# A hybrid attention and pooling layer on one core: the first output product of the last unit moved between two projections, and five stages' row factors sent through memory

## The chip, the cores and the metric

The kernel runs on one core of a Trainium2 chip. The metric is device microseconds of one execution. Three runs of the kernel before took 1174.0, 1173.38 and 1174.05 us; the median is 1174.0.

## What is computed

One layer on x of 4096 tokens by 1024 channels, in fp32. Normalised x goes through one combined projection into q, k, v, two gates and the input of a pooling group. The q, k, v feed attention of 8 query heads (2 key heads) inside a band of 128 tokens to both sides, with a learned bias and a sink. Attention and pooling, each times its gate, are joined and go through the output projection, whose normalised result is added to x. The core of the reference:

```python
h = rmsnorm(x, pre_norm_g[l])
proj = jnp.einsum('bsd,de->bse', h, w_in[l])
q, k, v, g_a, u_p, g_p = jnp.split(proj, splits, axis=-1)
...
a = banded_attention(q, k, v, rel_bias, attn_sink[l]) * jax.nn.silu(g_a)
p = multiscale_pool(u_p, pool_w[l], pool_scale[l]) * jax.nn.silu(g_p)
mixed = jnp.einsum('bse,ed->bsd', jnp.concatenate([a, p], axis=-1), w_out[l])
x = x + rmsnorm(mixed, post_norm_g[l])
```

with `rmsnorm(x, g) = x * rsqrt(mean(x*x) + eps) * g`. The factor rsqrt(...) is one number per token, here called the row factor.

## The kernel before

**Precision.** An fp32 operand is carried as two fp16 pieces, a high one and a low one (the rest). A product of two such operands takes three matmuls: high by high, high by low, low by high. "Low" instructions on VectorE or POOL make the second piece by a subtraction. The large products are further cut by a scheme of seven products for eight (names "11", "12", "22" for plain products, "s1" to "s4" for products of sums).

**Phase 1, up to about 481 us.** The tokens are cut into 8 stages of 512. The stages' steps (loads, squares, factors, operands, products) are put into a list by `do` and `ld`, each with an engine, a guessed duration and a due key, and `Steps.run` (line 78) orders them: at each point it takes the engine that is free first and, of the steps ready there, the one with the smallest due key. The order that comes out is the program's order on each engine. `prepare(m)` (line 968) adds what stage m needs before its products: four blocks of x with tokens on partitions are loaded, ScalarE squares and sums them (`square`), POOL takes the power −1/2 (`root`, into `rs4`, 128 tokens by 4 columns), TensorE spreads the factor (`spread_all`, line 445): x for the products is loaded with channels on partitions, so the factor has to stand along the free axis of all 128 partitions, and four fp32 products of `rs4`'s columns with a unit matrix bring it there, in PSUM. Then `norm` on VectorE multiplies x by gain and factor, and `x_operands` splits the result.

**Phase 2, from 481 us.** Units of 256 tokens are walked downward, 15 to 0 (`U` = 15 is the last unit of the sequence, the first to be done), and blocks of 128 tokens, 31 to 0, with them. `due(t, fn, ...)` collects all steps with a time written by hand; sorted by that time they are issued, and each engine works through its own in that order. The opening, unit 15, is written as one table of TensorE's steps and lists for the others (from line 1815); `at_` counts from the opening's start.

The steps that matter here, b a block, half one of two groups of heads, u a unit:

- `proj_k`, `proj_v`, `proj_q` (u): projections on TensorE; `keep_k`, `keep_v`, `keep_q`: ScalarE writes the high half, VectorE the low half (line 1230).
- `scores(b, half)` on TensorE; then `soft` places `logits` (VectorE, line 1308), `exps` (ScalarE, 1319), `denominators` (VectorE, 1326 and 1329), `probs` (ScalarE, 1341) and `rests` (VectorE, 1349), which write the tile `pn`, and `turn` (line 1358), a DMA transpose of `pn` into `pt` issued on SP.
- `values(b)` (line 1451) multiplies `pt` of half 0 and then of half 1 with the values `vv`; each half needs its own transpose.
- `gate(b)` (VectorE, 1475) takes the result out of PSUM; `sum1`, `sum3`, `sum2` (VectorE, 1536 to 1542) build the operands of the products of sums.
- `product(u, name, o, tag)` (line 1601) is one of the output products; its operand comes from `cast` (ScalarE and POOL, 1503 and 1507). `begin` (ScalarE, 1619) copies "11" out of its bank before "12" adds into it; `gain11` (VectorE, 1629) reads that bank last, and "s2" then overwrites it.
- Loads on SP: `load_wo` (1671), `pool_in` (1530), `load_ga` (1432), `load_xr` (1648), `load_x` (1226).

All of the DMAs of phase 2 are issued by SP, in its program order.

Of the kernel before, what the change touches and what calls it, by code (L numbers as in the profile page):

```python
# [8 lines left out]
F32 = mybir.dt.float32  # L9
# [8 lines left out]
P = 128  # L18
# [3 lines left out]
T = 512  # L22
NM = S // T
NB = S // P
# [15 lines left out]
O11, O12, O21, O22, OT1, OT2, OT4, OT3 = range(8)  # L40
# [16 lines left out]
class Steps:  # L57
# [28 lines left out]
    def run(self):  # L86
        n_steps = len(self.steps)
        users = [[] for _ in range(n_steps)]
        open_deps = []
        for n, s in enumerate(self.steps):  # L90
            open_deps.append(len(s[5]))
            for d in s[5]:
                users[d].append(n)
        ready = [0.0] * n_steps
        begun = [None] * n_steps
        free = dict.fromkeys(("PE", "DVE", "ACT", "POOL", "SP"), 0.0)
        dma_free = 0.0
        waiting = {e: [] for e in free}
        for n in range(n_steps):
            if not open_deps[n]:  # L100
                waiting[self.steps[n][0]].append(n)
        left = n_steps
        while left:
            best = None
            for e, ns in waiting.items():
                if ns:
                    t = max(free[e], min(ready[n] for n in ns))
                    if best is None or t < best[0]:
                        best = (t, e)
# [25 lines left out]
def hybrid_layer(ctx: ExitStack, tc, io, out):  # L135
    nc = tc.nc
# [4 lines left out]
    dram = ctx.enter_context(tc.tile_pool(name="dram", bufs=1, space=DRAM))  # L141
# [8 lines left out]
    mhalf = const.tile([P, 1], F32, name="mhalf")  # L150
# [12 lines left out]
    gs = const.tile([P, 1], F32, name="gs")  # L163
# [10 lines left out]
    epss = const.tile([P, 1], F32, name="epss")  # L174
    psc = const.tile([P, 4], F32, name="psc")

    f_row = dram.tile([NH, 512], F32, name="f_row")
    f_scr = dram.tile([NH, FR + 1, NF], F32, name="f_scr")
    x_scr = dram.tile([NU, P, 2, 2, HK, UT], F16, name="x_scr")
# [30 lines left out]
    with ExitStack() as actx:  # L210
        pa = actx.enter_context(tc.tile_pool(name="pa", bufs=1))
# [8 lines left out]
        ident = pa.tile([P, P], F32, name="ident")  # L220
        onesf = pa.tile([P, P], F32, name="onesf")
        edge = pa.tile([P, 4, 16], F32, name="edge")
        rs4 = pa.tile([P, 4], F32, name="rs4")
        xn1 = pa.tile([P, D], F32, name="xn")
        sqt = [pa.tile([P, D], BF16, name=f"sq{i}") for i in range(2)]
        ssq = [pa.tile([P, 4], F32, name=f"ssq{i}") for i in range(2)]
# [73 lines left out]
        V, G, A = nc.vector, nc.gpsimd, nc.scalar  # L300
# [61 lines left out]
        bc = {}  # L362
# [76 lines left out]
        def spread(m, i):  # L439
            nc.tensor.matmul(  # L440
                bc[m][:, i * P : (i + 1) * P], rs4[:, i : i + 1].to_broadcast([P, P]), ident,
                start=True, stop=True, skip_group_check=True,
            )

        def spread_all(m):
            bc[m] = psa.tile([P, T], F32, name=f"bc{m}", tag=f"wup{m % 2}")
            for i in range(4):
                spread(m, i)

        def n_view(m, c):  # L450
            return NT[:, (c % 2) * D : (c % 2 + 1) * D].rearrange("p (b t) -> p b t", b=2)
# [47 lines left out]
        for c in range(HK):  # L499
            do("ACT", act(512), -5 + 0.1 * c, first_square, c,  # L500
               r=[f"n0.{c}.0"], w=[f"xsq{c}"])
# [450 lines left out]


        def pads():
            V.memset(ubuf[:, :, 0:16], 0.0)
            V.memset(ubuf[:, :, T + 16 : T + 24], 0.0)

# [7 lines left out]
        sum_weights(UU, sw[:, 8:9], "u4", M1 + 8, 3.0, "DVE")  # L965
        sum_weights(GA, sw[:, 4:5], "a4", M1 + 27, 3.0, "DVE")

        def prepare(m):
            key = start(m) - 55
            b = m % 2  # L970
            for i in range(4):
                xn, k = (xn1, "xn") if m > 1 or i % 2 == 0 else (NT[:, 2 * D : 3 * D], "ts")
                t = key - 9 + 3 * i if m > 1 else 20 + i
                ld(t - 3, xn, x_blk[BPM * m + i], 0.5, w=[k])
                do("ACT", 1.3, t, square, m, i, xn, w=[k, f"ssq{m % 2}.{i}"])
            do("POOL", 1.0, key + 3, root, m, slice(0, 4), r=[f"ssq{m % 2}.{i}" for i in range(4)] + ["mhalf"],
               w=["rs4", "rs0", "rs1"])
            do("PE", 1.2, key + 5, spread_all, m, r=["rs4", "ident"], w=[f"wup{m % 2}"])
            for c in range(HK):
                k = key + 14 + 9 * c  # L980
                n = f"n1.{c % 2}"
                ld(k - 9, n_view(m, c), xT[c][:, :, m], 0.5,
                   w=[n] + ([f"xsq{i}" for i in range(HK)] if m == 1 and c < 2 else []))
                for h in range(2):
                    do("DVE", dve(512), k + h, norm, m, c, h, r=["gs", f"wup{m % 2}"], w=[n])
                x_operands(m, c, k + 2, "DVE")
            if m < NM - 1:
                for u in range(2):
                    do("SP", 0.45, key + 55 + 4 * u,
                       lambda u=u: nc.sync.dma_start(x_scr[2 * m + u], xb[b][:, u]),  # L990
                       r=xkeys(m, "b"), dma=3.5)
# [796 lines left out]
    for t, fn, *args in (  # L1788
        (0.0, proj_k, U, 2),
        (2.6, proj_v, U),  # L1790
        (5.4, proj_q, U, 0, 0),
        (10.8, proj_q1, U, 1, 0, 1),
        (13.5, scores, NB - 1, 0),
        (14.3, proj_q1, U, 1, 1, 1),
        (17.0, proj_k, U - 1, 2),
        (19.7, scores, NB - 1, 1),
        (20.6, proj_v, U - 1),
        (23.4, proj_q1, U - 1, 0, 0, 0),
        (26.1, scores, NB - 2, 0),
        (27.2, proj_q1, U - 1, 0, 1, 0),  # L1800
        (29.9, proj_q1, U - 1, 1, 0, 1),
        (32.6, scores, NB - 2, 1),
        (33.7, proj_q1, U - 1, 1, 1, 1),
        (36.4, values, NB - 1, 0),
        (38.4, product, U, "22", OT4, 2),
        (41.0, scores, NB - 3, 0),
        (42.0, proj_k, U - 2, 1),
        (44.7, proj_v, U - 2),
        (47.5, scores, NB - 3, 1),
        (48.4, product, U, "11", O11, 0),  # L1810
        (51.1, values, NB - 2, 1),
        (53.1, product, U, "12", O21, 0, True),
        (55.7, scores, NB - 4, 0),
        (56.7, proj_q, U - 2, 0, 1),
        (62.1, product, U, "s2", OT2, 0),
        (64.7, values, NB - 3, 1),
        (66.7, scores, NB - 4, 1),
        (67.6, proj_q, U - 2, 1, 0),
        (73.0, product, U, "s3", OT3, 1),
        (75.6, product, U, "s1", OT1, 0),  # L1820
    ):
        at_(t, fn, *args)
# [3 lines left out]
    soft(NB - 2, 0, 27.2, 27.8, 31.1, 31.6, 32.2, 34.5)  # L1826
    soft(NB - 2, 1, 34.4, 35.0, 38.3, 38.8, 39.4, 41.7)
    soft(NB - 3, 0, 42.0, 42.6, 45.9, 46.4, 47.0, 49.3)
    soft(NB - 3, 1, 50.1, 50.7, 54.0, 54.5, 55.1, 57.4)
    soft(NB - 4, 0, 59.4, 60.0, 63.2, 63.7, 64.3, 67.0)  # L1830
    softmax(NB - 4, 1, 67.6)

# [10 lines left out]
    at_(38.35, keep_q, U - 1, 1)  # L1843
    at_(38.37, gate, NB - 1)
    cast(41.0, 41.6, U, "11", a11, G)
    at_(46.3, keep_k, U - 2)
    at_(47.2, keep_v, U - 2)
    at_(50.5, begin, U)
    at_(53.1, gate, NB - 2)
    at_(53.2, sum1, U)  # L1850
    at_(54.1, sum3, U)
    at_(57.1, sum2, U)
    cast(58.0, 58.7, U, "s2", a11, G)
    at_(58.1, square, U, 0, 0, 0)
# [256 lines left out]
```

## Time and profile before

| | |
|---|---|
| profiled execution | 1173.47 us |
| its span, first to last instruction | 1171.7 us |
| mean granted TensorE clock | 0.998 |
| TensorE busy | 1154.8 us, 14420 matmuls |
| VectorE, ScalarE, POOL busy | 935.8, 703.3, 312.5 us |

Times in rows are microseconds from the span's start unless marked ns. PE is TensorE, PEld its weight loads, DVE VectorE, ACT ScalarE, SP the engine that issues the DMAs. In a row of the timeline stand start, duration, engine, line, operation, tiles written and read, shapes and how many like it follow in a piece; in brackets how long the engine stood idle before it and what ended that. An L with a number is a line of the kernel before.

### The profile page before, as it was taken

The numbers are of one execution on the slowest core, as the hardware profiler recorded it, in microseconds if no ns is written. First come the engines' busy times: TensorE is split into PE (matmuls) and PEld (weight loads), VectorE is DVE, ScalarE is ACT, GpSimd is POOL, SyncE is SP. The second block draws the span as 40 slices with busy tenths as digits, with TensorE's granted clock in tenths as the row PEclk, the third lists the DMA queues.
The fourth block names the chain that finished last, engine by engine and source line by source line (L and its number), as shares of the span: only waits on it lengthen the run. The fifth ranks groups of instructions, "written<-read, shape, count | busy, mean of one in ns | idle before, by whom it ended". The sixth has DMA issues, their size and how long they took to land. (4 is left out here: it accounts for less than half of the span.)

```text
span 1171.7 us, 34178 instructions
## 1 busy us (share of the span) xinstructions
PE 1154.8 (99%) x14420; PEld 889.6 (76%) x14420; DVE 935.8 (80%) x1864; ACT 703.3 (60%) x1460; POOL 312.5 (27%) x310
## 2 busy tenths in 40 slices
PE   7999999999999999999999999999999999999997
PEld 6998888998888888886667676676666767767643
DVE  6889997798688984558978877977787787797787
ACT  6876555557454542256676666666667666666672
POOL 0002111110110100201534433532543443353231
PEclk9999999999999999999999999999999999999999
DMA  9545587679457474299975886786787587686684
GB/s 345 211 126 183 168 268 245 181 250 289 155 176 243 149 195 137 74 279 229 250 183 138 197 202 134 198 187 183 164 190 180 139 200 197 133 196 161 175 213 145
DMA packets 291290, 224.67 MB, mean 192 GB/s; under 512 B 210576, under 2 KB 249744, under 8 KB 286528
## 3 DMA queue, kind: packets, MB, share of 16 engines
q1 hardware_dynamic: 291136, 222.48, 69.6%
q8 instruction: 113, 1.85, 0.7%
q14 instruction: 41, 0.34, 0.1%
HBM read 113.37 MB, written 60.33 MB: 148 GB/s over the span
## 5 line engine op out<-in xcount | busy, mean ns | idle before, releaser
L669 PEld LDWEIGHTS <-wq 128*128 128x128 f16 x4104 | 401.0, 98 | 53.0 <-issue 3.3
L669 PE MATMUL y<-xt,wq 128*128 128x256 f16 x1512 | 203.8, 273 | 0.1
L1319 ACT ACTIVATE p<-p,nm 128x385 f32<-128x385 f32 (+1 forms) x256 | 152.8, 599 | 36.3 <-POOL p L1302 20.4
L1240 PE MATMUL aq<-xb,xb 128*128 128x256 f16 x1024 | 173.4, 273 | 0.1
L1601 PE MATMUL ms<-wo,ys 128*128 128x512 f16 x720 | 162.7, 379 | 0.3 <-DVE mo L1640 0.3
L1349 DVE SCALAR_TENSOR_TENSOR pn<-p,rd,pn 128x384 f16<-128x384 f32 (+1 forms) x256 | 157.3, 665 | 5.9 <-ACT pn L1341 5.9
L1308 DVE CUSTOM_DVE_ANT_0 p<-s,nt,nsink 128x384 f32<-128x384 f32 (+1 forms) x256 | 155.9, 665 | 1.8 <-PE s L1285 1.7
L1240 PEld LDWEIGHTS <-xb 128*128 128x128 f16 x1280 | 125.2, 98 | 22.5 <-issue 6.3
L1240 PE MATMUL aq<-xb,xt 128*128 128x256 f16 x512 | 139.6, 273 | 0.0
L1341 ACT ACTIVATE pn<-p,rd 128x384 f16<-128x384 f32 (+1 forms) x256 | 134.5, 596 | 4.0 <-issue 1.1
L1601 PEld LDWEIGHTS <-ys 128*128 128x128 f16 x720 | 69.2, 98 | 81.6 <-issue 2.9
L1601 PE MATMUL m<-wo,y 128*128 128x512 f16 x540 | 121.8, 379 | 0.0
L304 POOL TENSOR_TENSOR yt<-yt,sg 128x512 f32<-128x512 f32 (+2 forms) x32 | 49.7, 1554 | 265.6 <-DVE yt L307 215.0
L1601 PEld LDWEIGHTS <-y 128*128 128x128 f16 x540 | 51.4, 98 | 63.4 <-issue 3.1
L1635 POOL TENSOR_TENSOR mo<-mo,gpost 128x512 f32<-128x512 f32 x39 | 63.8, 1635 | 94.6 <-ACT jkb L1624 93.4
L669 PE MATMUL plain<-xb,wq 128*128 128x256 f16 x576 | 67.0, 273 | 3.9 <-DVE wq L307 2.4
L1240 PEld LDWEIGHTS <-xt 128*128 128x128 f16 x640 | 62.6, 98 | 8.7 <-issue 0.4
L669 PE MATMUL v<-xt,wq 128*128 128x256 f16 x504 | 68.6, 273 | 0.6 <-DVE cc L304 0.6
L669 PE MATMUL x<-xb,wq 128*128 128x256 f16 x504 | 68.4, 273 | 0.6 <-DVE ubuf L307 0.5
L669 PE MATMUL y<-xb,wq 128*128 128x256 f16 x504 | 68.8, 273 | 0.0
L669 PE MATMUL v<-xb,wq 128*128 128x256 f16 x504 | 68.6, 273 | 0.0
L1451 PEld LDWEIGHTS <-vv 128*64 128x64 f16 (+1 forms) x2256 | 55.1, 109 | 12.2 <-issue 8.0
(214 smaller groups left out, 1935.3 us busy)
## 6 DMA issues: line engine op xcount, KB each, us to landing
nt<-in_xT SPq DMA_DIRECT2D x28, 512.0 KB, 4.7
x_scr<-xb SPq DMA_DIRECT2D x14, 1024.0 KB, 7.0
xb<-x_scr SPq DMA_DIRECT2D x14, 1024.0 KB, 7.4
xr<-in_x SPq DMA_DIRECT2D x28, 512.0 KB, 4.5
out<-xr SPq DMA_DIRECT2D x28, 512.0 KB, 2.6
xn<-in_x SPq DMA_DIRECT2D x27, 512.0 KB, 5.1
ga_scr<-cc SPq DMA_DIRECT2D x64, 128.0 KB, 3.1
raw<-in_w_out SPq DMA_DIRECT2D x16, 512.0 KB, 4.9
```

Of the source, the lines that this page charges most:

```text
L304: eng.tensor_tensor(out=out, in0=in0, in1=in1, op=op)
L669: nc.tensor.matmul(b[:, s], wq[:, slot[q, op], wv, s, k, :], x[:, xv, k, :], start=(first and k + s + wv + xv == 0), stop=(last and k == H ...
L1240: nc.tensor.matmul(acc, w[:, j, k, :], x[:, kh, v, kt, :], start=(n == 0), stop=(n == 3 * KT - 1),)
L1308: nc.vector.tensor_tensor_reduce(out=p_t[b, half][:, hh, :nk], in0=s_t[jj][:, gg, :nk], in1=bias[:, h, lo : lo + nk], scale=negc[:, h : h ...
L1319: nc.scalar.activation(p[:, hh, : nk + 1], p[:, hh, : nk + 1], AF.Exp, bias=nm_t[b, half][:, hh : hh + 1], scale=-1.0, accum_out=den_t[b, ...
L1341: nc.scalar.activation(prob_view(b, half)[:, 0, i], p_t[b, half][:, i, :nk], AF.Copy, scale=rd_t[b, half][:, i : i + 1],)
L1349: nc.vector.scalar_tensor_tensor(out=pn4[:, 1, i], in0=p_t[b, half][:, i, :nk], scalar=rd_t[b, half][:, i : i + 1], in1=pn4[:, 0, i], op0= ...
L1451: nc.tensor.matmul(o_t[b][side][a, half], v_t[ku][ks, vi, kt, a], pt[b, half][ks, pi, g, :, kb - kbs[0], (LOW, TOP)[side]], start=start, s ...
L1601: nc.tensor.matmul(z_t[u, tag], y[:, k, yi, :], wo[o][:, wi, k, :], start=(n == 0 and acc is None), stop=(n == 3 * HK - 1), skip_group_che ...
L1635: eng.tensor_tensor(out=mo, in0=mo, in1=gpost[:, cs], op=ALU.mult)
```

## The change

It has two parts.

The first: for stages 3 to 7 (`MS` = 3) `spread_all` is left out. In its place VectorE copies `rs4` into four columns of a tile of 128x32 and transposes it in blocks of 32x32, SP stores the four rows of each block into a scratch row in memory (four DMAs) and loads that row broadcast to all partitions (one DMA) into `rows`, one SBUF tile; `norm` reads it in place of the PSUM tile. The loads of x blocks, squares and root of these stages have due keys 20 us earlier. For the latency of the two transfers the planner gets an engine "NET" with steps of 12 and 8 us that issue nothing.

The second: in unit 15's opening product "11" goes between `proj_k` and `proj_v` of unit 13, product "12" ahead of `values` of block 30, and the steps of ScalarE, VectorE and SP near them get other times.

```diff
@@ class Steps, run
-        free = dict.fromkeys(("PE", "DVE", "ACT", "POOL", "SP"), 0.0)
+        free = dict.fromkeys(("PE", "DVE", "ACT", "POOL", "SP", "NET"), 0.0)
@@ phase 1
+        def rows_turn(m):
+            V.tensor_copy(turned[0][:, :4], rs4)
+            V.transpose(out=turned[1], in_=turned[0])
+
+        def rows_store(m):
+            for i in range(4):
+                nc.sync.dma_start(
+                    rs_scr[m, i * P : (i + 1) * P].rearrange("(r c) -> r c", c=32),
+                    turned[1][i::32, :],
+                )
+
+        def rows_load(m):
+            bc[m] = rows
+            nc.sync.dma_start(
+                rows, rs_scr[m].rearrange("(o t) -> o t", o=1).to_broadcast([P, T])
+            )
@@ pads
+            V.memset(turned[0], 0.0)
@@ prepare
-                t = key - 9 + 3 * i if m > 1 else 20 + i
+                t = key - 9 - early + 3 * i if m > 1 else 20 + i
...
-            do("PE", 1.2, key + 5, spread_all, m, r=["rs4", "ident"], w=[f"wup{m % 2}"])
+            if m < MS:
+                spread_key = f"wup{m % 2}"
+                do("PE", 1.2, key + 5, spread_all, m, r=["rs4", "ident"], w=[spread_key])
+            else:
+                spread_key = "rsp"
+                do("DVE", 0.5, key - 12, rows_turn, m, r=["rs4"], w=["turned"])
+                do("SP", 1.8, key - 12, rows_store, m, r=["turned"], w=["rs_scr"])
+                do("NET", 12.0, key - 12, lambda: None, w=["rs_scr"])
+                do("SP", 0.45, key - 8, rows_load, m, r=["rs_scr"], w=["rsp"])
+                do("NET", 8.0, key - 8, lambda: None, w=["rsp"])
@@ unit 15, the table of TensorE
         (42.0, proj_k, U - 2, 1),
-        (44.7, proj_v, U - 2),
-        (47.5, scores, NB - 3, 1),
-        (48.4, product, U, "11", O11, 0),
-        (51.1, values, NB - 2, 1),
-        (53.1, product, U, "12", O21, 0, True),
+        (44.7, product, U, "11", O11, 0),
+        (47.3, proj_v, U - 2),
+        (50.1, scores, NB - 3, 1),
+        (51.0, product, U, "12", O21, 0, True),
+        (53.6, values, NB - 2, 1),
         (55.7, scores, NB - 4, 0),
@@ unit 15, the others (soft: times of logits, exps, denominators, probs, rests, turn)
-    soft(NB - 3, 1, 50.1, 50.7, 54.0, 54.5, 55.1, 57.4)
+    soft(NB - 3, 1, 51.1, 51.7, 55.0, 55.5, 56.1, 58.4)
...
-    at_(46.3, keep_k, U - 2)
-    at_(47.2, keep_v, U - 2)
-    at_(50.5, begin, U)
-    at_(53.1, gate, NB - 2)
-    at_(53.2, sum1, U)
-    at_(54.1, sum3, U)
+    at_(47.4, begin, U)
+    at_(50.1, keep_k, U - 2)
+    at_(50.2, keep_v, U - 2)
+    at_(55.7, gate, NB - 2)
+    at_(55.75, sum1, U)
+    at_(56.5, sum3, U)
```

The loads near there keep their times:

```python
at_(49.4, load_ga, NB - 3)
at_(57.5, load_wo, OT1)
at_(57.6, load_wo, O22)
at_(58.0, pool_in, U - 1, 0)
at_(58.1, load_ga, NB - 4)
at_(58.2, load_xr, U, 1)
at_(58.2, load_xr, U, 0)
```

What this does to the order is seen at two places. The first is SP in unit 15's opening, from the transpose of block 29, half 0, on (`pt29_0` is that transpose's target, `wo` a weight block, `yf` pooling's result, `gb` a gate, `xr` a block of x for the residual). In the kernel before:

```order
L1358 DMA_TRANSPOSE pt29_0_7037<-pn29_0_6964 128x24x128
L1432 DMA gb29_7039<-ga_scr_96 128x512
L1358 DMA_TRANSPOSE pt29_1_7259<-pn29_1_7152 128x24x128
L1671 DMA wo4_6065<-w_scr_98 128x4096
L1671 DMA wo3_6064<-w_scr_98 128x4096
L1530 DMA yf0_14_7265<-yp_scr_95 128x512
L1432 DMA gb28_7269<-ga_scr_96 128x512
L1648 DMA xr30_7272<-in_x 128x1024
L1648 DMA xr31_7274<-in_x 128x1024
L1358 DMA_TRANSPOSE pt28_0_7449<-pn28_0_7309 128x24x128
```

In the changed kernel (whose lines are 33 further on):

```order
L1391 DMA_TRANSPOSE pt29_0_7003<-pn29_0_6942 128x24x128
L1465 DMA gb29_7005<-ga_scr_97 128x512
L1704 DMA wo4_6080<-w_scr_99 128x4096
L1704 DMA wo3_6079<-w_scr_99 128x4096
L1563 DMA yf0_14_7278<-yp_scr_96 128x512
L1465 DMA gb28_7282<-ga_scr_97 128x512
L1681 DMA xr30_7285<-in_x 128x1024
L1681 DMA xr31_7287<-in_x 128x1024
L1391 DMA_TRANSPOSE pt29_1_7289<-pn29_1_7161 128x24x128
L1391 DMA_TRANSPOSE pt28_0_7464<-pn28_0_7324 128x24x128
```

The transpose of block 29, half 1, has moved from ahead of six loads to behind them.

The second place is VectorE at the same time: from the reciprocals of (29,1) to `gain11` (`at30` the gated block 30, `s1_15` the result of sum1, `mo15_0` that of `gain11`). Before:

```order
L1475 SCALAR_TENSOR_TENSOR at30_7144<-o30_7054,gaf_78,gb30_6730 128x4x64
L1475 SCALAR_TENSOR_TENSOR at30_7144<-p30_7053,gaf_78,gb30_6730 128x4x64
L1536 TENSOR_TENSOR s1_15_7147<-at30_7144,yf0_15_6101 128x512
L1326 TENSOR_SCALAR den29_1_7042<-den29_1_7042 128x4
L1329 RECIPROCAL rd29_1_7043<-den29_1_7042 128x4
L1539 TENSOR_TENSOR at30_7144<-at30_7144,at31_6795 128x512
L1349 SCALAR_TENSOR_TENSOR pn29_1_7152<-p29_1_7044,rd29_1_7043,pn29_1_7152 128x384 x4
L1542 TENSOR_TENSOR at31_6795<-s1_15_7147,at31_6795 128x512
L1629 TENSOR_TENSOR mo15_0_7047<-m11_15_7023,gpost_6069 128x512
```

After:

```order
L1359 TENSOR_SCALAR den29_1_7073<-den29_1_7073 128x4
L1362 RECIPROCAL rd29_1_7074<-den29_1_7073 128x4
L1508 SCALAR_TENSOR_TENSOR at30_7211<-o30_7085,gaf_78,gb30_6745 128x4x64
L1508 SCALAR_TENSOR_TENSOR at30_7211<-p30_7084,gaf_78,gb30_6745 128x4x64
L1569 TENSOR_TENSOR s1_15_7214<-at30_7211,yf0_15_6116 128x512
L1382 SCALAR_TENSOR_TENSOR pn29_1_7161<-p29_1_7075,rd29_1_7074,pn29_1_7161 128x384
L1572 TENSOR_TENSOR at30_7211<-at30_7211,at31_6810 128x512
L1382 SCALAR_TENSOR_TENSOR pn29_1_7161<-p29_1_7075,rd29_1_7074,pn29_1_7161 128x384
L1575 TENSOR_TENSOR at31_6810<-s1_15_7214,at31_6810 128x512
L1382 SCALAR_TENSOR_TENSOR pn29_1_7161<-p29_1_7075,rd29_1_7074,pn29_1_7161 128x384 x2
L1662 TENSOR_TENSOR mo15_0_6994<-m11_15_6927,gpost_6084 128x512
```

The two gates and the three sums, of which two gates and a sum stood ahead of the reciprocals and one sum behind pn, now all stand between the reciprocals and the last pn. Ahead of these rows, the low halves of unit 13's keys and values (one before the first and one before the second of the four pn of (29,0)) now follow all four pn of (29,0), ahead of the logits of (29,1).

In phase 1 SP's order at the first of the changed stages, stage 3, becomes (`rs_scr` the scratch row; `ga_scr` and `yp_scr` results of phase 1, `x_scr` operands of x, `nt` and `xn` loads of x):

```order
L459 DMA rs_scr_92<-turned1_117 4x32 x4
L890 DMA yp_scr_96<-yt0_123 128x8
L891 DMA yp_scr_96<-yt0_123 128x3x128
L896 DMA yp_scr_96<-yt0_123 128x120
L1023 DMA x_scr_95<-xb0_66 128x4096 x2
L131 DMA nt_69<-in_xT 128x2x512
L131 DMA xn_118<-in_x 128x1024
L890 DMA yp_scr_96<-yt1_124 128x8
L891 DMA yp_scr_96<-yt1_124 128x3x128
L896 DMA yp_scr_96<-yt1_124 128x120
L726 DMA ga_scr_97<-cc2_128 128x2x128 x2
L466 DMA rows_115<-rs_scr_92 128x512
```

The load of the row stands eleven rows behind its stores; the other rows but the `rs_scr` and `rows` ones are those of before in another order.

More of the change, by code (lines that the diff above doesn't have):

```diff
@@ L175, in hybrid_layer @@
     psc = const.tile([P, 4], F32, name="psc")
+    rs_scr = dram.tile([NM, T], F32, name="rs_scr")
     f_row = dram.tile([NH, 512], F32, name="f_row")
@@ L223, in hybrid_layer @@
         rs4 = pa.tile([P, 4], F32, name="rs4")
+        rows = pa.tile([P, T], F32, name="rows")
+        turned = [pa.tile([P, 32], F32, name=f"turned{i}") for i in range(2)]
         xn1 = pa.tile([P, D], F32, name="xn")
@@ L966, in hybrid_layer @@
         sum_weights(GA, sw[:, 4:5], "a4", M1 + 27, 3.0, "DVE")
+        MS = 3
         def prepare(m):
             key = start(m) - 55
+            early = 20 * (m >= MS)
             b = m % 2
@@ L972, in prepare @@
                 xn, k = (xn1, "xn") if m > 1 or i % 2 == 0 else (NT[:, 2 * D : 3 * D], "ts")
-                t = key - 9 + 3 * i if m > 1 else 20 + i
+                t = key - 9 - early + 3 * i if m > 1 else 20 + i
                 ld(t - 3, xn, x_blk[BPM * m + i], 0.5, w=[k])
                 do("ACT", 1.3, t, square, m, i, xn, w=[k, f"ssq{m % 2}.{i}"])
-            do("POOL", 1.0, key + 3, root, m, slice(0, 4), r=[f"ssq{m % 2}.{i}" for i in range(4)] + ["mhalf"],
+            do("POOL", 1.0, key + 3 - early, root, m, slice(0, 4), r=[f"ssq{m % 2}.{i}" for i in range(4)] + ["mhalf"],
                w=["rs4", "rs0", "rs1"])
-            do("PE", 1.2, key + 5, spread_all, m, r=["rs4", "ident"], w=[f"wup{m % 2}"])
+            if m < MS:
[8 more added lines that the diff above has]
+                do("NET", 8.0, key - 8, lambda: None, w=["rsp"])
             for c in range(HK):
@@ L984, in prepare @@
                 for h in range(2):
-                    do("DVE", dve(512), k + h, norm, m, c, h, r=["gs", f"wup{m % 2}"], w=[n])
+                    do("DVE", dve(512), k + h, norm, m, c, h, r=["gs", spread_key], w=[n])
                 x_operands(m, c, k + 2, "DVE")
```

## The prediction

> **What bounds the kernel now.** I read first the page's busy times, then the waits of TensorE, then the timeline around the places that the diff touches.
>
> ```profile
> PE 1154.8 (99%) x14420; PEld 889.6 (76%) x14420; DVE 935.8 (80%) x1864; ACT 703.3 (60%) x1460; POOL 312.5 (27%) x310
> ```
>
> TensorE works in 99% of the span. So a matmul taken off it is time won, and each microsecond for which it has to wait is time lost, unless a wait that stands there already takes it up. Two answers on its waits follow: of phase 1 (148 to 480 us), and of the last unit's opening (520 to 600 us). Columns: line, what it waited for, us in all, times, longest.
>
> ```profile
> PE v L669 <- DVE cc L304: 0.6, 1, 0.6
> PE o L1451 <- DMA pt<-pn: 1.5, 1, 1.5
> PE ms L1601 <- DVE mo L1640: 0.3, 1, 0.3
> ```
>
> In phase 1 there is one wait of 0.6 us. In the opening there is one of 1.5 us, at values(30), for a DMA transpose, and one of 0.3.
>
> **Part one: the row factors.** What stood on TensorE is one group of eight matmul records (four fp32 products, two passes each) between two groups of the projection:
>
> ```profile
> 375.45 1.06 PE L440 MATMUL bc<-ident,rs 128*128 128x128 f32 x8
> 376.34 0.82 PE L669 MATMUL y<-xt,wq 128*128 128x256 f16 x6
> L890 DVE COPY sg<-sg 128x32 f32<-128x32 f32 x7 | 1.2, 170 | 0.0
> ga_scr<-cc SPq DMA_DIRECT2D x64, 128.0 KB, 3.1
> 250.00:400.00 150.00, 149.40 (x1370) 133.88 (x1368) 124.75 (x193) 79.66 (x110) 22.35 (x16) 1.00 0.67 215
> ```
>
> 376.34 − 375.45 = 0.89 us of TensorE for a spread. Five stages (3 to 7) lose theirs: 5 × 0.89 = **4.45 us** off the engine that is never free.
>
> In its place, per stage, come a copy of 128x4 and a 32x32-wise transpose on VectorE; the nearest row is the 128x32 copy, 0.17 us, so about 0.34 us a stage and 1.7 in all. VectorE is busy 124.75 of 150 us in the window quoted last (its columns: the stretch, its length, busy PE, PEld, DVE, ACT, POOL, clock, DMA share, GB/s), so 25 us are free there: I cost them at nothing. If they met the one VectorE-bound wait of 0.6 us, they would add 0.34 us there. SP issues four stores of 4x32 and one broadcast load per stage, and the load waits until the stores have landed; the stores of `ga_scr` (the row: kilobytes each, us to landing) land after 3.1 us, so SP may stand for about 3 us, with the loads of x behind it. The squares and the root are 20 us earlier and so cover that latency (two trips of 3 to 6 us), and VectorE's multiplies by the factor keep their number and size and read it from SBUF in place of PSUM, which I cost at nothing: no row tells the two apart here, and the 25 us hide a difference either way. That phase 1 had 0.6 us of waits says that x operands were never the last thing. From both sides: all of this is hidden (0), or it returns a wait like the 0.6 above in some stages (+1). Against a gain beyond 0.89 a spread nothing stands but the reading error of the groups' starts; the part is −3.5 to −5.5, and I take −4.45.
>
> **Part two: the opening of unit 15.** The timeline of TensorE shows the pieces that change places:
>
> ```profile
> 537.47 2.76 PE L1601 MATMUL m<-wo,y 128*128 128x512 f16 x12
> 540.16 0.25 PE L1451 MATMUL o<-pt,vv 128*64 128x128 f16 x2
> 542.51 0.25 PE L1451 MATMUL o<-pt,vv 128*64 128x128 f16 x2 [1.49 <-DMA pt<-pn]
> 543.76 2.76 PE L1601 MATMUL m<-wo,y 128*128 128x512 f16 x12
> 546.46 0.93 PE L1285 MATMUL s<-k_all,q 64*32 64x288 f16 x48
> 552.57 2.75 PE L1601 MATMUL ms<-wo,ys 128*128 128x512 f16 x12
> 555.25 0.25 PE L1451 MATMUL o<-pt,vv 128*64 128x128 f16 x2
> 555.95 0.22 PE L1451 MATMUL o<-pt,vv 128*64 128x128 f16 x2
> 557.17 0.93 PE L1285 MATMUL s<-k_all,q 64*32 64x288 f16 x48
> ```
>
> These are product "11" (537.47), values(30) (540.16; its second half at 542.51 after the wait), product "12" (543.76), scores(28,0) (546.46), product "s2" (552.57), values(29) (first half 555.25, second half 555.95), scores(28,1) (557.17). Product "11" now comes ahead of proj_v and scores(29,1), which the table gives 2.8 and 0.9 us: 537.47 − 3.7 = 533.8 is its new start, and product "12" stands where values(30) stood, at 540.2 or a little later. The halves start 0.70 apart where nothing is late (555.25 to 555.95); at values(30) they are 2.35 apart, so the wait costs 1.65 us. With "12" (2.7 us) ahead of values(30), the transpose has long landed: this wait goes, **−1.65**. What could take its place at once are the operands of the two products:
>
> ```profile
> 532.75 1.36 POOL L1507 TENSOR_TENSOR y<-at,y 128x512 f16<-128x512 f32 x1 [13.20 <-ACT y L1503]
> 540.53 0.57 ACT L1619 COPY mo<-m 128x512 f32<-128x512 f32 x1
> ```
>
> The low half of "11"'s operand is ready on POOL at 534.1, so "11" waits up to 0.3 us, with proj_v, scores(29,1) and "12" queued behind it. "12" adds into the bank that `begin` copies out on ScalarE (0.57 us). That copy may start as soon as "11" ends, at 536.5, and stands ahead of or between the probs of (29,0), of which each takes about 0.55; it is done by 539.9 and "12" follows at 540.2. I cost both at 0.2 us, with ends of 0 and 0.8. What is late next is the point of the forecast.
>
> values(29) needs two transposes, and the second one, of half 1, is moved past six loads on SP's queue. Before, SP did this:
>
> ```profile
> 546.06 0.58 SPq L1432 DMA_DIRECT2D gb<-ga_scr  x1
> 548.87 3.64 SPq L1358 DMA_TRANSPOSE pt<-pn  x1
> 552.55 1.07 SPq L1671 DMA_DIRECT2D wo<-w_scr  x2
> 560.68 5.40 SPq L1358 DMA_TRANSPOSE pt<-pn  x1
> ```
>
> The turn of (29,1) was due at 57.4, ahead of the loads (57.5 to 58.2); it is now due at 58.4, behind them. The loads wait for nothing new (two weight blocks of 1024 KB, two of 256 KB, two of 512 KB, 3584 KB together), so SP issues them as soon as the load of gb is out, at 546.06 + 0.58 = 546.64 in place of 552.55: 5.9 us earlier. What a transpose does behind such loads the trace shows once, with (28,0) at 560.68, beside (29,1) ahead of them:
>
> ```profile
> L1358 SPq DMA_TRANSPOSE pt<-pn x1: 3637/3637/3637, 548.9 to 548.9; - x1
> DMA to landing us min/median/max: 5.5/5.5/5.5
> L1358 SPq DMA_TRANSPOSE pt<-pn x1: 5397/5397/5397, 560.7 to 560.7; - x1
> DMA to landing us min/median/max: 8.8/8.8/8.8
> 556.00:558.00 2.00, 2.00 (x101) 1.58 (x96) 1.27 (x3) 1.74 (x4) 0.00 (x0) 1.00 1.00 422
> 562.00:564.00 2.00, 2.00 (x18) 1.56 (x16) 1.79 (x6) 1.96 (x8) 1.99 (x2) 1.00 1.80 341
> ```
>
> Ahead of loads: 5.5 us from issue to landing. Behind them: 8.8. The loads move at 422 GB/s with the queue's engines full (share 1.00 at 556 to 558), 3584 KB take 8.7 us, and with 1.4 to 2 us of start they end about 10.8 us after the first issue: 563.3 before, inside the last window quoted, where the rate falls off and the transposing begins. (28,0) landed at 560.68 + 8.8 = 569.5, 6.2 us after that. In the changed kernel the loads drain by 546.64 + 10.8 = 557.4. It may be up to 0.8 earlier, since the low halves of unit 13's keys and values no longer stand among the pn whose transpose goes out ahead of them (below); I take half of it, 557.0.
>
> When is the transpose issued? Its input is written by VectorE:
>
> ```profile
> 541.57 0.68 DVE L1308 CUSTOM_DVE_ANT_0 p<-s,nt,nsink 128x384 f32<-128x384 f32 x1
> 544.67 0.19 ACT L1319 ACTIVATION_READ_ACCUMULATOR p<-p,nm 128x1 f32 x1
> 544.88 0.69 DVE L1536 TENSOR_TENSOR s<-at,yf 128x512 f32<-128x512 f32 x1
> 546.59 2.20 DVE L1349 SCALAR_TENSOR_TENSOR pn<-p,rd,pn 128x384 f16<-128x384 f32 x4 [0.15 <-ACT pn L1341]
> 550.67 0.69 DVE L1629 TENSOR_TENSOR mo<-m,gpost 128x512 f32<-128x512 f32 x1 [1.27 <-ACT jkb L1624]
> ```
>
> (In the second row ScalarE ends the last exponent of (29,1), at 544.86.) The logits of (29,1) start at 541.57 before; by the new order unit 13's keys and values are kept behind all four pn of (29,0) and not among them, so that VectorE, which before filled its wait for ScalarE's probs with them, does two low halves of 128x256 by themselves, about 0.4 us each (a pn of 128x384 takes 2.20 / 4 = 0.55): 0.8 us later, so the exponents end at 545.7 and the reciprocals at 546.1. Then come two gates (0.4 each), three sums (the next start follows 0.62 behind the 544.88 row's) and the four pn (0.53 apart), with the sums now among the pn: 546.1 + 0.8 + 1.9 + 2.1 = 550.9 for the end of pn, in place of 546.59 + 2.20 = 548.8, and the transpose is issued at 551.0. The loads are then 6 us from drained, so it waits in the queue: landing at 556.6 + 3.5 (5.5 for a transpose with a free queue, less the 2 us of start, which lie beside the loads) to 557.4 + 6.2, that is **560.1 to 563.6, and I take 561.6**, which is 557.0 + 4.6, between the two.
>
> TensorE gets there earlier: "s2" could start at 552.57 − 1.65 + 0.2 = 551.1, but gain11 on VectorE (the 550.67 row, which reads the bank that "s2" overwrites) comes behind pn, at about 551.9. So values(29) starts at 554.7 and wants its second half at 555.4. It waits 561.6 − 555.4 = 6.2 us. scores(28,1) then starts 557.17 − 555.95 = 1.22 us after the landing, at 562.8 in place of 557.17: **+5.6** (from +4.1 at 560.1 to +7.6 at 563.6), with the −1.65 in it. The 0.3 us wait on `mo` behind it goes, −0.3.
>
> **Part three: the clock.** TensorE has not stood for 6 us since its start. What a pause does is seen at both ends:
>
> ```profile
> 1.07 5.73 PE L402 MATMUL idle<-ones 128*128 128x128 bf16 x52 [1.07 <-DVE ones L325]
> 7.35 2.40 PE L402 MATMUL idle<-ones 128*128 128x128 bf16 x40
> 1160.21 5.34 PE L1573 MATMUL z<-wo,xt 128*128 128x512 f16 x24
> 1167.00:1168.00 1.00, 0.00 (x0) 0.00 (x0) 0.88 (x2) 0.00 (x0) 0.34 (x1) 0.81 0.00 0
> ```
>
> The last matmul ends at 1160.21 + 5.34 = 1165.55; over 1167 to 1168 the granted clock is 0.81, so if it fell to a half it fell at 1167.6, 2 us into the pause. At the start 52 matmuls took 110 ns each, later ones 60: 52 × 50 ns = 2.6 us lost until full speed was back. A pause of 6.2 us should cost the same again, **+2.6** (0 if the clock holds, 3 at most).
>
> The Trainium skill, "TensorE: Matmul & The Clock Gate", section "What's actually happening", has a free-running window of 3413 ns: an idle one halves the clock, and about 3.4 us of work restore it. An estimate from that page is 1.7 us lost, and the sum would be 0.9 us lower; the start of this trace shows the larger loss.
>
> **The sum.** −4.45 + 5.6 + 2.6 − 0.3 = +3.45 us on the profiled execution's own 1173.47, so 1176.9; that execution is 0.5 under the median of 1174.0, so **1177.4** on the median's scale.
>
> **Rivals.** (a) The transpose is not held: its packets come between those of the loads and it lands 5.5 us after its issue, at 556.5. Place: second half of values(29). Then scores(28,1) starts at 557.7, 0.5 later than before, and the sum is −4.45 + 0.5 − 0.3 = −4.25: **1169.7**. Deciding point: a landing up to 558.3 keeps the kernel over 0.2% faster (+2.4 at that place). For it: no row shows a transpose passing loads, but the loads may start later than I have them. The Trainium skill, "DMA: Bandwidth & Descriptors", section "Queues, rings and completion order", speaks against it: on each DMA engine descriptors are consumed in ring order, and SP owns one ring on each. The 8.8 us of (28,0) agree. (b) It is held, but the clock stays up, or the loads drain sooner: −4.45 + 5.6 − 0.3 = +0.85 gives 1174.9, and with a landing at 559.2 (+3.3 in place of +5.6) 1172.5. For it: the trace has no long pause from which work resumed but the start. (c) The row factors come late, or SP's stand delays the x loads, and phase 1 gives back what it won: 1177.4 + 4.45 = 1182. Against it: the plan starts the squares 20 us earlier, and the two landings take at most 12.
>
> **How the numbers follow.** Forecast 50%, (c) 5%, (b) 25%, (a) 20%. The forecast's own ends are −5.5 + 4.1 + 0 − 0.3 (1172.3) and −3.5 + 7.6 + 3 (1181.1). The range takes in (b) and the point of (a): 1169 to 1181. A measurement of this kernel can tell about 0.2%, 2.35 us: faster is under 1171.65, slower over 1176.35. Faster has (a), 0.20; within 0.2% has (b), 0.25; slower has the forecast and (c), 0.55.
>
> **What would show it.** TensorE's waits: none at values(30), one of 5 to 8 us at values(29) for `pt<-pn`, in a page whose clock drops for a slice. SP's timeline: six loads from 546 or so, the transpose behind them at 551, 9.1 to 12.6 us to landing. The L440 group has 24 records in place of 64, and phase 1 ends about 4.5 us earlier. I am wrong if that landing is under 6 us, if the wait at values(29) is under 2, or if phase 1 has new waits of over 1 us.

## The result, and the profile after

| | before | after |
|---|---|---|
| median of 11 runs each | 1173.67 us | 1177.3 us |
| profiled execution | 1173.47 us | 1176.39 us |
| its span | 1171.7 us | 1174.6 us |
| mean granted TensorE clock | 0.998 | 0.996 |

The ratio is 1.0028 with a 95% interval of 1.0018 to 1.0038: the changed kernel is slower by 0.28%, 3.6 us by the medians and 2.9 us by the two profiled executions.

The page's busy times and the waits of TensorE over the whole span, after (line, what it waited for, us in all, times, longest; those of the program's first 27 us and others of up to 0.5 us are left out):

```profile
PE 1150.6 (98%) x14380; PEld 885.1 (75%) x14380; DVE 937.2 (80%) x1875; ACT 702.6 (60%) x1460; POOL 314.8 (27%) x310
...
PE o L1484 <- DMA pt<-pn: 6.3, 2, 5.3
...
PE aq L1273 <- DVE at L1508: 1.4, 1, 1.4
PE s L1318 <- issue: 1.2, 3, 0.6
```

TensorE works 4.2 us less (1154.8 to 1150.6, 40 matmul records fewer) and the span is 2.9 us longer: it now waits, once for 5.3 us for a transpose, and once for 1.4 us for VectorE's gate of block 30, which was in no row before.

The timeline of TensorE after: the spread of stage 2, which is the last one that both kernels have, then unit 15's opening; the pieces of the opening are those that the prediction shows of before:

```profile
96.13 1.06 PE L443 MATMUL bc<-ident,rs 128*128 128x128 f32 x8
...
525.50 0.93 PE L1318 MATMUL s<-k_all,q 64*32 64x288 f16 x48
...
535.29 2.76 PE L1634 MATMUL m<-wo,y 128*128 128x512 f16 x12
537.99 0.25 PE L1484 MATMUL o<-pt,vv 128*64 128x128 f16 x2
...
539.97 1.08 PE L1318 MATMUL s<-k_all,q 64*32 64x288 f16 x48
542.50 0.27 PE L1273 MATMUL aq<-xb,xb 128*128 128x256 f16 x1 [1.45 <-DVE at L1508]
...
547.74 2.75 PE L1634 MATMUL ms<-wo,ys 128*128 128x512 f16 x12
550.42 0.25 PE L1484 MATMUL o<-pt,vv 128*64 128x128 f16 x2
...
556.62 0.32 PE L1484 MATMUL o<-pt,vv 128*64 128x128 f16 x2 [5.34 <-DMA pt<-pn]
...
558.82 1.64 PE L1318 MATMUL s<-k_all,q 64*32 64x288 f16 x48
...
565.83 5.34 PE L1634 MATMUL ms<-wo,ys 128*128 128x512 f16 x24
...
571.96 2.76 PE L1634 MATMUL ms<-wo,ys 128*128 128x512 f16 x12
```

and five rows of before that the prediction did not need:

```profile
94.99 1.06 PE L440 MATMUL bc<-ident,rs 128*128 128x128 f32 x8
...
530.18 0.93 PE L1285 MATMUL s<-k_all,q 64*32 64x288 f16 x48
...
547.32 0.28 PE L1240 MATMUL aq<-xb,xb 128*128 128x256 f16 x1
...
563.42 5.34 PE L1601 MATMUL ms<-wo,ys 128*128 128x512 f16 x24
...
569.92 1.46 PE L1601 MATMUL ms<-wo,ys 128*128 128x512 f16 x6 [0.30 <-DVE mo L1640]
```

Read the starts of the same piece against each other:

| piece | before | after | difference so far |
|---|---|---|---|
| spread of stage 2 | 94.99 | 96.13 | +1.14 |
| scores(29,0), first piece of the opening shown | 530.18 | 525.50 | −4.68 |
| scores(28,0), behind values(30) | 546.46 | 539.97 | −6.49 |
| first piece of proj_q(13) | 547.32 | 542.50 | −4.82 |
| second half of values(29) | 555.95 | 556.62 | +0.67 |
| scores(28,1) | 557.17 | 558.82 | +1.65 |
| product "s3" | 563.42 | 565.83 | +2.41 |
| product "s1" | 569.92 | 571.96 | +2.04 |
| end of span | 1171.7 | 1174.6 | +2.9 |

The first 1.14 us are lost in the program's first 13 us (the first spread starts at 12.15 before and at 13.28 after), and that start differs from profile to profile: in the experiments below the spread of stage 2 starts at 94.75 and 95.46 with the old phase 1 (4 and 2), at 94.78 and 95.98 with the new one (5 and 9). From that spread to scores(29,0) it is 435.19 us before and 429.37 after: 5.82 us less, the worth of the row factors. The missing wait at values(30) won 1.8 more; the gate of block 30 took 1.7 back at once; the transpose cost 5.5; slow matmuls behind it 1.7; the wait for `mo` gave 0.4. The last 0.9 lie far behind, in pauses "issue" of the scores (1.2 us in all, 0.2 before), which differ from profile to profile: 1.5 us in the first experiment below, 0.7 in the ninth.

SP's timeline shows why the transpose is late, and the windows what it does to the clock (columns as in the prediction: clock, DMA share and GB/s are the last three):

```profile
541.16 0.59 SPq L1465 DMA_DIRECT2D gb<-ga_scr  x1
541.79 1.76 SPq L1704 DMA_DIRECT2D wo<-w_scr  x2
...
544.55 0.92 SPq L1681 DMA_DIRECT2D xr<-in_x  x2
546.56 13.46 SPq L1391 DMA_TRANSPOSE pt<-pn  x2
```

```profile
552.00:554.00 2.00, 0.00 (x0) 0.00 (x0) 1.44 (x3) 2.00 (x5) 0.00 (x0) 0.99 1.11 337
554.00:556.00 2.00, 0.00 (x0) 0.00 (x0) 2.00 (x3) 1.59 (x4) 1.36 (x2) 0.50 1.23 278
556.00:558.00 2.00, 1.38 (x24) 1.25 (x23) 0.27 (x1) 0.00 (x0) 2.00 (x3) 0.50 0.26 50
558.00:560.00 2.00, 2.00 (x68) 1.46 (x72) 1.01 (x3) 0.10 (x1) 0.52 (x1) 0.50 1.17 215
560.00:562.00 2.00, 2.00 (x29) 1.36 (x14) 2.00 (x7) 1.92 (x6) 1.16 (x1) 0.80 0.89 182
```

The loads start at 541.79, the transpose is issued at 546.56 behind them and TensorE gets it at 556.62, 10 us later. In that pause the clock falls to 0.50 and is back within 560 to 562.

### The profile page after: what moved, and what is told of

It is laid out like the page before. It is cut to its first block, busy times and chain, and to the rows that moved or that the text cites. A ratio compares the mean times of both kernels' runs of the same rounds, so it can differ in the third digit from the quotient of the medians.

```text
span 1174.6 us, 34143 instructions
## 1 busy us (share of the span) xinstructions
PE 1150.6 (98%) x14380; PEld 885.1 (75%) x14380; DVE 937.2 (80%) x1875; ACT 702.6 (60%) x1460; POOL 314.8 (27%) x310
```

## The experiments

All times are medians; before ran beside each group (1173.52, 1173.26 and 1173.43 us).

**1 and 2: each part alone.** The first is the changed kernel with all lines of unit 15 (the table, soft, the others) as before; the core of it:

```diff
-        (44.7, product, U, "11", O11, 0),
-        (47.3, proj_v, U - 2),
-        (50.1, scores, NB - 3, 1),
-        (51.0, product, U, "12", O21, 0, True),
-        (53.6, values, NB - 2, 1),
+        (44.7, proj_v, U - 2),
+        (47.5, scores, NB - 3, 1),
+        (48.4, product, U, "11", O11, 0),
+        (51.1, values, NB - 2, 1),
+        (53.1, product, U, "12", O21, 0, True),
```

The second is the changed kernel with everything of phase 1 as before:

```diff
-            if m < MS:
-                spread_key = f"wup{m % 2}"
-                do("PE", 1.2, key + 5, spread_all, m, r=["rs4", "ident"], w=[spread_key])
...
+            do("PE", 1.2, key + 5, spread_all, m, r=["rs4", "ident"], w=[f"wup{m % 2}"])
```

> Row factors of stages 3 to 7 through memory, unit 15's opening as before. Theory (the two parts add up, each TensorE spread is worth its 0.89 us and memory hides the rest): 4.4 to 4.9 us less than before, about 1169.0, phase 1 without new waits of TensorE, the wait at values(30) of 1.5 us still there. Rival (the extra DMAs or the earlier squares cost something of phase 1 or later): less than 3 us won.

> The new opening of unit 15, spreads on TensorE as before. Theory (the opening loses by itself: wait for the transpose behind six loads, clock down, gate of block 30 late): 6 to 8 us more than before, about 1181, wait at values(29) of 5 to 6 us, clock 0.50 in a stretch of some microseconds. Rival (the loss comes of both parts together, by DMAs or stages shifted against each other): less than 4 us more.

Row factors alone: 1168.65 us, ratio 0.9953 (0.9939 to 0.9967), 4.9 us less. The view of TensorE's waits lists none from 148 to 480 us, and one of 2.2 us at values(30). From the spread of stage 2 to scores(29,0) it is 429.39 us (95.33 to 524.72), as in the changed kernel; of the 5.8 us won there, the longer wait at values(30) gives 0.7 back. Opening alone: 1181.5 us, ratio 1.0064 (1.0052 to 1.0077), 8.0 us more, with the two waits of the changed kernel:

```profile
PE o L1451 <- DMA pt<-pn: 6.1, 1, 6.1
PE aq L1240 <- DVE at L1475: 1.4, 1, 1.4
```

−4.9 + 8.0 = +3.1, beside +3.6 measured for both: the parts add up, and they have different signs. The kernel with both hides a gain of 0.4% behind a loss of 0.7%.

**3 and 4: the transpose's place in the queue, by itself.** In the changed kernel the six loads were put behind the transpose of (29,1); in the kernel before, only that transpose was put behind the loads.

```diff
-    at_(57.5, load_wo, OT1)
-    at_(58.0, pool_in, U - 1, 0)
-    at_(58.1, load_ga, NB - 4)
-    at_(58.2, load_xr, U, 1)
-    at_(58.2, load_xr, U, 0)
-    at_(57.6, load_wo, O22)
+    at_(58.5, load_wo, OT1)
+    at_(58.6, pool_in, U - 1, 0)
+    at_(58.65, load_ga, NB - 4)
+    at_(58.7, load_xr, U, 1)
+    at_(58.7, load_xr, U, 0)
+    at_(58.55, load_wo, O22)
```

```diff
-    soft(NB - 3, 1, 50.1, 50.7, 54.0, 54.5, 55.1, 57.4)
+    soft(NB - 3, 1, 50.1, 50.7, 54.0, 54.5, 55.1, 58.4)
```

> The changed kernel with one thing other: the six loads of unit 15's opening come 0.45 to 1 us later in the plan, so that the transpose of (29,1) stands ahead of them on SP. Theory (the place in the queue is the cause): issue at 546.6 as now, landing 5 to 6 us later at 552, a wait at values(29) of about 1 us in place of 5.3, no fall of the clock, 6 to 7.5 us less than the changed kernel, about 1170. Rival (the transpose is late because VectorE's sums stand among its inputs): landing after 554 and less than 3 us won.

> The kernel before with one thing other: the transpose of (29,1) due at 58.4 in place of 57.4, behind the six loads, and nothing of the products moved. Theory (the place in the queue is the cause): loads from 546.6, landing about 14.8 us behind the first of them (what the changed kernel shows), near 561.4 where TensorE wants it at 556, a wait of 5 to 6 us, clock down, 6 to 8 us more than before, about 1180.5. Rival (VectorE's order in the changed opening is the cause): within 2 us of before.

The changed kernel with the transpose first: 1169.45 us, ratio to before 0.9967 (0.9956 to 0.9978), 7.9 us less than the changed kernel. Its SP and TensorE:

```profile
546.30 3.63 SPq L1391 DMA_TRANSPOSE pt<-pn  x1
549.97 1.07 SPq L1704 DMA_DIRECT2D wo<-w_scr  x2
```

```profile
542.23 0.27 PE L1273 MATMUL aq<-xb,xb 128*128 128x256 f16 x1 [1.45 <-DVE at L1508]
551.85 0.25 PE L1484 MATMUL o<-pt,vv 128*64 128x128 f16 x2 [0.84 <-DMA pt<-pn]
```

The issue is at the same time as in the changed kernel (546.30, 546.56), VectorE's order is the same, and TensorE has the result at 551.85 in place of 556.62: 5.5 us behind the issue in place of 10.1. The kernel before with the transpose late: 1181.05 us, ratio 1.0064 (1.0048 to 1.008), 7.5 us more. Its loads start at 546.55, the transpose is issued at 550.21, and TensorE waits:

```profile
561.34 0.32 PE L1451 MATMUL o<-pt,vv 128*64 128x128 f16 x2 [5.66 <-DMA pt<-pn]
```

14.8 us behind the first load, as in the changed kernel (541.79 to 556.62). One number in one line, 57.4 to 58.4, makes nearly all of the opening's loss. VectorE's order as the cause is out.

**5: is the pause paid a second time, through the clock?** The pause was filled with matmuls whose result is overwritten.

```diff
         for half in range(2):
+            if half == 1 and b == NB - 3:
+                for _ in range(22):
+                    nc.tensor.matmul(
+                        s_t[0][:, 0], wo[O11][:, 0, 0, :P], wo[O11][:, 0, 0, :],
+                        start=True, stop=True, skip_group_check=True,
+                    )
```

> The changed kernel with 22 matmuls of 128x512 on a scores bank that nobody needs then, put between the two halves of values(29), where TensorE waits 5.3 us for the transpose (their result is overwritten by the next scores). They take about 22 x 0.227 = 5.0 us, so they end before the transpose lands. Theory (the pause lowers the granted clock, and slow matmuls behind it cost 1.7 us by the durations of the pieces that follow it): no fall of the clock, the second half of values(29) lasts 1.2 us in place of 2.2, 1.5 to 1.8 us less than the changed kernel, about 1175.6. Rival (the pieces are slow for another cause, or the added matmuls come on top): 0 to 5 us more.

1174.66 us, ratio to before 1.0016 (1.0008 to 1.0025): 2.6 us less than the changed kernel by the medians. But this interval overlaps that of the changed kernel (1.0018 to 1.0038), and both kernels' runs scatter over 4 us: that the kernel as a whole became faster is not shown. The pieces tell more:

```profile
524.15 0.93 PE L1318 MATMUL s<-k_all,q 64*32 64x288 f16 x48
...
549.86 4.92 PE L1493 MATMUL s<-wo 128*128 128x512 f16 x22
556.92 0.25 PE L1484 MATMUL o<-pt,vv 128*64 128x128 f16 x2 [2.14 <-DMA pt<-pn]
...
558.17 0.93 PE L1318 MATMUL s<-k_all,q 64*32 64x288 f16 x48
559.03 0.28 PE L1273 MATMUL aq<-xb,xb 128*128 128x256 f16 x1
...
564.28 5.34 PE L1640 MATMUL ms<-wo,ys 128*128 128x512 f16 x24
```

```profile
552.00:554.00 2.00, 2.00 (x11) 0.91 (x10) 2.00 (x4) 2.00 (x5) 0.72 (x1) 1.00 1.35 118
```

The second half of values(29) takes 558.17 − 556.92 = 1.25 us in place of 558.82 − 556.62 = 2.20, and from its start to "s3" it is 7.36 us in place of 9.21; the clock reads 1.00 in each window from 550 to 562. So the pause is paid a second time, with 1.85 us by these pieces, and filling it saves that. A wait of 2.1 us that was left did not lower the clock.

The kernel did not keep the saving in this profile. From scores(29,0) to "s3" it takes 40.13 us (524.15 to 564.28), the changed kernel 40.33: 0.2 us less. The transpose came 32.77 us behind scores(29,0), 31.12 in the changed kernel, and these 1.65 us ate the rest; in the window 552 to 554 the DMA engines moved 118 GB/s, 337 in the changed kernel. Whether the filling causes that stays open. Most of the 1.7 us by which the two profiled executions differ (1176.39 and 1174.66) lies ahead of the opening, where scores(29,0) starts 1.35 us earlier.

**6: what else holds the new opening.** Gate and pn first on VectorE, the transpose at 57.2.

```diff
-    soft(NB - 3, 1, 51.1, 51.7, 55.0, 55.5, 56.1, 58.4)
+    soft(NB - 3, 1, 51.1, 51.7, 55.0, 55.1, 55.2, 57.2)
...
-    at_(55.7, gate, NB - 2)
-    at_(55.75, sum1, U)
-    at_(56.5, sum3, U)
+    at_(54.9, gate, NB - 2)
+    at_(55.1, sum1, U)
+    at_(57.08, sum3, U)
```

> The changed kernel with VectorE's order in unit 15's opening other: gate of block 30 ahead of the denominators of (29,1), the four pn of (29,1) ahead of sum3 and sum2, and the transpose due at 57.2, ahead of the six loads, which keep their times. Theory (what is left of the opening's loss are the waits for the gate, 1.4 us, and for a transpose issued at 546.5): pn ends about 544.4, the transpose is issued there and lands by 550, the wait at values(29) goes, the one for the gate falls to 0.4, and 0.5 to 1.5 us are won over the version with the transpose first, about 1168.4. Rival (the opening is held by something else, gain11 or the operand of product s2): within 0.4 us of that version, 1169.5.

1170.13 us, ratio 0.9971 (0.996 to 0.9983), 0.7 above the version with the transpose first. The theory lost, and the number is above the rival's too (within 0.4 of 1169.5); the place is the rival's, gain11 and the operand of product "s2":

```profile
PE ms L1634 <- DVE mo L1662: 1.3, 1, 1.3
PE aq L1273 <- DVE mo L1673: 0.4, 1, 0.4
PE ms L1634 <- DVE mo L1673: 0.3, 1, 0.3
PE aq L1273 <- DVE at L1508: 0.2, 1, 0.2
```

```profile
546.04 0.69 DVE L1662 TENSOR_TENSOR mo<-m,gpost 128x512 f32<-128x512 f32 x1 [1.27 <-ACT jkb L1657]
546.78 2.75 PE L1634 MATMUL ms<-wo,ys 128*128 128x512 f16 x12 [1.32 <-DVE mo L1662]
```

The wait for the transpose is gone and that for the gate has fallen to 0.2 us. Now "s2" waits 1.3 us and gain11 (L1662) is the last to come, the wait that I had expected of the changed kernel. VectorE is not full there: it has itself stood 1.27 us, until ScalarE ended `jkb`, its squares of the same bank. They follow the cast of "s2"'s operand, which starts at 544.80, with the end of sum2 on VectorE (544.77). POOL's half of that operand ends at 546.65, only 0.1 us ahead of gain11. So both ways to "s2" begin at sum2, and up to sum2 VectorE has no gap of more than 0.2 us from the logits of (29,1) on (536.74). The changed kernel's order made TensorE wait for the gate, this one for gain11; an order with `jkb` ahead of the cast was not run.

**7 and 8: more stages.** The same kernel with `MS = 2` and `MS = 1`.

> The version before this one (gate and pn first) with stage 2's row factors through memory too. Theory (each spread is worth its 0.89 us as long as the row comes in time): 0.9 us less than that version. Rival (in the early stages the loads of weights and x stand close and the row is late): 0.5 us less to 3 us more, with a new wait of TensorE between 60 and 150 us.

> The same from stage 1 on (only stage 0 keeps its spread). Theory: 1.8 us less than the version from stage 3. Rival (the row is late in stage 1): more than that version, with a wait of TensorE between 30 and 100 us.

From stage 2: 1169.6 us, ratio 0.9968 (0.9956 to 0.9979), 0.5 less than experiment 6, within the scatter. From stage 1: 1178.8 us, ratio 1.0045 (1.0032 to 1.0059), 8.7 more. The waits of phase 1, first of stage 2's version (100 to 160 us), then of stage 1's (60 to 150):

```profile
PE x L689 <- DVE ubuf L310: 0.7, 1, 0.7
PE v L689 <- DVE cc L307: 0.5, 1, 0.5
```

```profile
PE y L689 <- DVE xb L307: 7.1, 2, 4.9
```

With `MS` = 3 only the first stands there, with 0.5. From stage 2 the second wait and 0.2 on the first nearly eat the spread's 0.89; from stage 1 TensorE stands 7.1 us for operands of x, and behind each of the two pauses the clock is at a half (two windows, columns as above):

```profile
105.56 1.01 PE L689 MATMUL y<-xb,wq 128*128 128x256 f16 x4 [4.89 <-DVE xb L307]
111.88 0.37 PE L689 MATMUL y<-xb,wq 128*128 128x256 f16 x1 [2.24 <-DVE xb L307]
```

```profile
106.00:108.00 2.00, 2.00 (x11) 1.40 (x10) 2.00 (x4) 0.00 (x0) 0.00 (x0) 0.50 0.56 156
112.00:114.00 2.00, 2.00 (x11) 1.41 (x10) 1.85 (x3) 0.97 (x2) 0.00 (x0) 0.50 0.58 76
```

In that run SP issues stage 2's stores at 93.1 and the row's load at 108.0. Whether the row itself or the loads of x beside it are what comes late was not separated.

**9 and 10: the same lesson for the old wait.** The transpose of (30,1), which values(30) waits for in the kernel before, is itself issued behind a load of 1024 KB (`load_x`).

```diff
-    at_(36.5, load_x, U - 3)
+    at_(41.75, load_x, U - 3)
```

> Row factors through memory, the old opening, and the load of unit 12's x (1024 KB, wanted some 40 us later) due at 41.75 in place of 36.5, so that it stands behind the transpose of (30,1) on SP. Theory (the wait at values(30) is the place in the queue too: the transpose was issued at 529.1 behind that load, whose packets ran to 530, and landed at 537.7): landing 5 to 6 us behind the issue, at 535, wait at values(30) gone, 1.5 to 2.2 us less than the version with the row factors alone, about 1167. Rival (that transpose is slow for another reason, or the load then holds the next transpose): within 0.5 us of that version.

> The kernel before with that one load behind the transpose of (30,1). Theory: the wait of 1.5 us at values(30) goes, 1.2 to 1.7 us less than before, about 1172. Rival: no change.

With the row factors: 1168.09 us, ratio 0.9957 (0.9944 to 0.9969), the lowest median of all, 0.6 less than without, a third of what was expected; the ratios (0.9953 without) show no gain at all, so the rival's "within 0.5 us" fits better. The wait fell from 2.2 to 0.8 us, but the transpose, now with no load right ahead of it, still took 7.2 us (issued at 529.75, used at 536.95). On the kernel before: 1175.22 us, ratio 1.0014 (1.0005 to 1.0023), 1.8 us **more**: a miss. Its waits (515 to 600 us):

```profile
PE o L1451 <- DMA pt<-pn: 3.1, 3, 1.5
```

0.7 at values(30), and new ones at values(29), 0.9, and values(28), 1.5. The load did not go away; it now stands ahead of the next transpose, whose issue takes 7.8 us, and the ones after it shift. Why the version with the row factors escapes that was not tried.

## Why the prediction was right, point by point

The forecast was 1177.4 us, slower; measured 1177.3. The sum for the profiled execution was +3.45, measured +2.9. Term by term:

- **Row factors, −4.45**: −5.82, from the spread of stage 2 to scores(29,0), outside the −3.5 to −5.5 that were given for it. The five spreads are 4.5 of it. The sum had nothing for pauses of TensorE that would go, which are the other 1.3: 0.6 us on `cc` in phase 1, 0.2 on `cc` at 481 us and smaller ones. What was costed at nothing cost nothing: five copies (0.16 us) and five transposes (0.21) on VectorE and 25 DMAs lie beside other work, and VectorE's multiplies take 0.74 us from SBUF as from PSUM. SP took 14 us from the stores of stage 3 (144.22) to the load of their row (158.23), more than the 12 of the prediction, but within the 20 us of head start.
- **The program's start, not in the sum**: +1.14, which differs from profile to profile. The two together are the −4.68 at scores(29,0), close to −4.45 by luck.
- **The wait at values(30), −1.65**: gone. But the step behind it, that "s2" could start 1.45 sooner, held only in part: proj_q(13) writes the bank that values(30) used, and waited 1.45 for the gate of block 30, now behind the denominators on VectorE. I had moved that gate in the sum for pn and not asked who waits for it. The prediction had a brake of about the same kind one piece later, gain11 ahead of "s2"; that one did not bite (gain11 ends at 547.4, "s2" starts at 547.74). So values(29) wanted its second half at 551.1, near the forecast (555.4 − 4.68 = 550.7), but behind another wait than the forecast's; this agreement is luck too.
- **The transpose behind six loads, landing 10.6 us behind its issue**: 10.1. Taken back by 4.68, the forecast's 561.6 is 556.9; TensorE went on at 556.62. Experiments 3 and 4 show the place in the queue as the cause, in both directions.
- **scores(28,1), +5.6**: +1.65 + 4.68 = +6.33, of which 1.0 belongs to the next term (2.20 − 1.22 for the second half of values(29)), so +5.35.
- **The clock, +2.6**: the right mechanism, too large. The pieces that follow the pause are longer by 1.0 (second half of values(29)), 0.57 (scores(28,1), from 558.82 to the next at 560.40; 1.01 before) and 0.19 (the rest to "s3"): 1.74. The loss had been taken from the program's start, where full speed took longer to come, and that row itself varies: the same 52 matmuls took 5.73 us before and 4.66 in the changed kernel.
- **The wait for `mo`, −0.3**: 2.41 − 2.04 = 0.37, gone.

Added up: −5.82 + 1.14 + 5.35 + 1.74 − 0.37 + 0.86 = +2.90. The mechanism of the loss is the one that was forecast, a transpose behind six loads and a slow clock behind the pause. The number came out because the row factors won 1.4 us more than forecast and the clock cost 0.9 less, while the start and the "issue" pauses, in no term of the sum, took 2.0 back; that the last digits agree is luck. The rivals: (a), a transpose that passes the loads, is out by experiment 4. (b), a pause without a fall of the clock, is out by the windows. (c), a late row, does not occur from stage 3 on, but does from stage 1 on (experiment 8).

On the clock the Trainium skill, "TensorE: Matmul & The Clock Gate", section "What's actually happening", gave the better price: the estimate from its window was 1.7 us, the pieces show 1.74, though the clock here stayed at a half for about 4.2 us of work and not for 3.4. On the queue the Trainium skill, "DMA: Bandwidth & Descriptors", section "Queues, rings and completion order", has the rule that on each DMA engine descriptors are consumed in ring order; experiments 3 and 4 agree with it.

## What to carry to other kernels

When a step's time in a plan is moved, look at every queue on which it leaves something: here one microsecond in the plan put a transpose behind 3584 KB of loads and cost more than five removed pieces of TensorE work brought. Before a wait is removed, follow the engine to its next two or three needs (bank, buffer, transfer); a wait that goes lets the next one appear, as in the two new orders of VectorE's work here, which made TensorE wait at two different places. Before two profiles are set against each other, take off what their starts differ by: 1.1 us here, a third of the measured change. A change of two parts wants two runs: the two had opposite signs, and the row factors alone are 0.47% faster than before.

## What the runs showed of the hardware beyond that

- A transpose that is issued into a full queue holds SP itself: its issue took 8.0 us in the changed kernel (13.46 for two in a row), 3.63 with a free queue.
- A pause of 5.3 us halved the granted clock (0.99 over 552 to 554 and 0.50 after, so it fell at 554, 2.7 us into it), and it was full again about 4 us after work resumed (0.80 over 560 to 562). With shorter pauses it can go either way: 2.16 us (experiment 1) and 2.14 (experiment 5) left it at 1.00, 2.24 us (experiment 8, 4 us behind a longer pause) took it to 0.50. In the program's start a pause of 2.35 us, ended by the same operand, was followed by 0.50 in experiments 1, 3, 7 and 9 and by 1.00 in the two kernels of this document.
- Matmuls of no use, put into a pause, kept the clock at 1.00 and took 1.85 us off the work behind it; that the whole kernel gains by it is not shown.
